# Hybrid decoder step on one core: gate squares summed before the ones product, low parts by adding DMAs, readouts on ScalarE

## The chip, the cores and the metric

The kernel runs on one core of one Trainium2 chip. The host lays arrays out and nothing more, and the program is launched once. The metric is the device time of that core in microseconds (us): before the change 984.8 us, the median of three runs from 984.1 to 984.87.

## The reference, cut to what matters

One inference step of a decoder trunk: 512 prompt tokens and 8 sampled tokens (520 columns in all) of width 1024 go through a feed-forward network (FFN), a mixer and a second FFN, each added to the residual stream `h`. The change lies in the mixer. Its parts:

```python
proj = h @ w_in
u_pool, z, xbc, dt_raw = jnp.split(proj, ...)        # 512, 1024, 1536, 16 columns
pool_out, new_pool = _pool_mix(u_pool, ...)
xbc_act, new_conv = _causal_conv(xbc, ...)
xs, Bm, Cm = jnp.split(xbc_act, ...)
y, h_new = _ssd_scan(xs_h, dt, A, Bm, Cm, h0, chunk)
y = y + d_skip[:, None] * xs_h
y = y.reshape(b, T, SSD_DIM) * jax.nn.silu(z)
yg = y.reshape(b, T, SSD_GROUPS, SSD_DIM // SSD_GROUPS)          # 2 groups of 512
yg = yg * lax.rsqrt(jnp.mean(yg * yg, axis=-1, keepdims=True) + EPS)
y = yg.reshape(b, T, SSD_DIM) * ssd_norm
cat = jnp.concatenate([pool_out, y], axis=-1)
return cat @ w_out, ...
```

For a sampled token the scan is one step: `y_off` is the old state (16 heads of 64 x 128) times the row `C` of its group, summed over the 128 state columns, and scaled by a decay.

## The kernel before, in words

Everything is feature-major: 128 features on the partitions, the 520 columns along them, taken in two halves of 260. Products are made in three passes: a weight and an input are each split into a high part, rounded to the type that TensorE multiplies in one pass (`F32R`), and the low rest; `mm3` (L121) then issues high x high (L122), high x low (L125) and low x high (L126).

A weight of 128 x 1024 is a unit. `load_unit` (L116) brings it with one DMA of SyncE into a half of a `raw` pair (two pairs, so four halves) and calls `split` (L101): ScalarE copies it to `whi` (L106), and VectorE subtracts to get `wlo` (L113). `whi` and `wlo` have three buffers each. `split` has a second way, which the FFNs' weights use for half of their columns: with `late` given, ScalarE writes the negated raw weight, rounded, into `wlo` (L109), and a DMA issued by GpSimd adds the weight from HBM to it (L110).

The mixer runs as stages from two written plans, CONV_PLAN and GATE_PLAN, and a last one that overlaps with the second FFN. The stages that matter here:

- `z` (`zproj`, L1046): eight units of the input projection for the gate z, 48 matmuls each, evacuated by VectorE into `zs`.
- `o`, `g`, `h` (`wout`, L1053): twelve units of the output weights, four for each third of the concatenated input: the pooling part `catp`, then gate groups 0 and 1 (`catg`). 48 matmuls each, added into `h` by VectorE (L1061).
- `A`, `B` (`ssd_a`, `ssd_b`): the scan, a chunk of 128 tokens of one group at a time. GpSimd makes `xw` (L1011), which the state product `pst` (L1024) reads, and scales the running state (L1033).
- `s` (`samples`, L1097): the readouts of sampled tokens. `sample(b, g)` (L906) loads a broadcast row C as `cb` and four state blocks as `h0`, and VectorE multiplies and sums each block in one instruction with an accumulator output into a column of `ysm` (L913): 16 calls, 64 instructions.
- `G` (`gate`, L1067): finishes `ysm` for the group (`sample_y`), takes the silu of z, adds the sampled tokens' readouts (L1075) and multiplies into `zs` (L1077).
- `H` (`gate_out`, L1079): ScalarE squares the group's four tiles of `zs` into `X` (L1083). `rstd` (L165) then lets TensorE multiply each by a matrix of ones and accumulate (L168), which sums over the partitions and puts the sum on all of them; a square root (L169) and a reciprocal (L170) follow. VectorE scales (L1090), ScalarE writes the high part of `catg` (L1091) and VectorE its low part (L1092).

The plans fix the order in which the stages are traced. A planner then simulates the program with its own costs and writes each engine's instruction order from that; on the chip, each engine runs its list in order. The instructions inside `keep_in_program_order` stay in traced order on their engine. What waits in an engine's list holds up all that stands behind it there, and this holds for DMAs too: SyncE's list issues the plain loads, GpSimd's list the adding ones.

Of the kernel before, what the change touches and what calls it, by code (L numbers as in the profile page):

```python
# [11 lines left out]
AF = mybir.ActivationFunctionType  # L12
ALU = mybir.AluOpType
# [3 lines left out]
P = 128  # L17
D = 1024
# [43 lines left out]
def tile_trunk_step(ctx: ExitStack, tc: tile.TileContext, ins: dict, outs: dict):  # L62
    nc = tc.nc
# [6 lines left out]
    wp = ctx.enter_context(tc.tile_pool(name="wp", bufs=3, side="right"))  # L70
# [24 lines left out]
    def raw_tile(name):  # L95
        if not half:
            t = raw_pair(name)
            half.extend([t[:, 1], t[:, 0]])
        return half.pop()

    def split(src, n, name, hp, nb, tags, late=None):  # L101
        hi, lo = (hp.tile([P, 1024], F32R, tag=t, bufs=nb, name=f"{t}_{name}")[:, :n] for t in tags)
        h, l = hi, lo
        if len(src.shape) == 3:
            h, l = (t.rearrange("p (j c) -> p j c", j=src.shape[1]) for t in (hi, lo))
        nc.scalar.copy(h, src)  # L106
        q = 0 if late is None else n - late.shape[1]
        if late is not None:
            nc.scalar.activation(out=lo[:, q:], in_=src[:, q:], func=AF.Copy, scale=-1.0)  # L109
            nc.gpsimd.dma_start(out=lo[:, q:], in_=late, accum_op=ALU.add)  # L110
        if late is None or q:
            s = slice(0, q) if late is not None else slice(None)
            nc.vector.tensor_tensor(out=l[:, s], in0=src[:, s], in1=h[:, s].bitcast(F32), op=ALU.subtract)  # L113
        return hi, lo

    def load_unit(src, n, name):  # L116
        raw = raw_tile(name)[:, :n]
        nc.sync.dma_start(out=raw, in_=src)
        return split(raw, n, name, wp, 3, ("whi", "wlo"))

    def mm3(ps, whi, wlo, xhi, xlo, start, stop, pin=False, **kw):  # L121
        first = nc.tensor.matmul(ps, whi, xhi, start=start, stop=False, **kw)  # L122
# [81 lines left out]
    class Ffn:  # L204
# [257 lines left out]
        def down(self, c, lo, hi, after):  # L462
            n = hi - lo
            banks, units = {}, {}

            def part(d, ks):
                if d not in units:
                    units[d] = load_unit(ins[f"w{self.i}d"][d, :, lo * P : hi * P], n * P, f"{self.i}d{d}_{c}")
                    banks[d] = ps[0].tile([P, 2, 512], F32, tag="BE", bufs=2, name=f"dn{self.i}_{d}_{c}")
                wh, wl = units[d]  # L470
                for b in range(2):
                    for k in ks:
                        g = self.g[lo + k]
                        mm3(banks[d][:, b, :HB], ws(wh, k), ws(wl, k), g[:, 0, b], g[:, 1, b], k == 0, k == n - 1)

            def done(d):
                for b, hs in enumerate(HALVES):
                    nc.vector.tensor_tensor(out=h[:, d, hs], in0=banks[d][:, b, :HB], in1=h[:, d, hs], op=ALU.add)
                    after(d, b, hs)

            part(0, range(n - 1))
            part(1, range(n - 1))
            part(0, range(n - 1, n))
            done(0)
            part(1, range(n - 1, n))
            done(1)
            for d in range(2, KD):
                part(d, range(n))
                done(d)
# [54 lines left out]
    for j in range(KD // 2):  # L544
        for d in (j, j + KD // 2):
            q = slice(NVEC + d * NT if d else 0, NVEC + (d + 1) * NT)
# [82 lines left out]
    todo, late = [], []  # L629
# [48 lines left out]
def mixer(tc, ins, outs, e):  # L678
    nc = tc.nc
    cst, act, wp, tmp, dr, pool = (e[x] for x in ("cst", "act", "wp", "tmp", "dr", "pool"))  # L680
    ones = e["ones"]
    bank, load_unit, mm3, ws, v, rstd, rstds, vec, h, nx2, raw_tile, open_f2, fin, fill = (
        e[x] for x in ("bank", "load_unit", "mm3", "ws", "v", "rstd", "rstds", "vec", "h", "nx2", "raw_tile",
                       "open_f2", "fin", "fill"))
# [19 lines left out]
    X = mp.tile([P, NX, NT], F32, tag="X", name="X")  # L704
# [1 line left out]
    npp = mp.tile([P, 4, PAST], F32, tag="npp", name="npp")  # L706
    ncp = mp.tile([P, 12, 3], F32, tag="ncp", name="ncp")

    def inproj(src, name):
        wh, wl = load_unit(src, D, f"in{name}")  # L710
        bs = [bank(f"in{name}{b}") for b in range(2)]
        for b, hs in enumerate(HALVES):
            for k in range(KD):
                mm3(bs[b][:, :HB], ws(wh, k), ws(wl, k), xh[:, k, hs], xl[:, k, hs], k == 0, k == KD - 1)
        return bs
# [111 lines left out]
    def pooling(g):  # L827
        w = WINDOWS[g]
        bs = inproj(ins["w_in"][12 + g], f"p{g}")
        U = cv[0].tile([P, LP], F32, tag="cu", bufs=6, name=f"PU{g}")  # L830
        us = U[:, SAMPLE_P:LP].rearrange("p (b j) -> p b j", j=16)
# [39 lines left out]
    ysm = mp.tile([P, NX, NS], F32, tag="ysm", name="ysm")  # L871
    sbc = mp.tile([P, 2, NS], F32, tag="sbc", name="sbc")
    junk = act.tile([P, NT], F32, tag="acc", name="junk")[:, :P]
    scr_bc = dr.tile([NS, 512], F32, name="scr_bc")

    def rows_bc(b, a, g):
        return scr_bc.rearrange("b (a g n) -> b a g n", a=2, g=2)[b, a, g].unsqueeze(0).to_broadcast([P, P])
# [28 lines left out]
    def sample(b, g):  # L906
        cb = tmp.tile([P, HB], F32, tag="ta", name=f"cb{b}{g}")[:, :P]
        nc.sync.dma_start(out=cb, in_=rows_bc(b, 1, g))
        h0 = mp.tile([P, 4, P], F32, tag="h0", bufs=4, name=f"h0_{b}{g}")
        nc.sync.dma_start(out=h0, in_=ins["state_ssm"][:, b, 4 * g : 4 * g + 4])  # L910
        for q in range(4):
            tc.keep_in_program_order(
                nc.vector.scalar_tensor_tensor(out=junk, in0=h0[:, q], scalar=1.0, in1=cb, op0=ALU.mult, op1=ALU.mult,  # L913
                                               accum_out=ysm[:, 4 * g + q, b : b + 1]))

    def sample_y(g):
        gs = slice(4 * g, 4 * g + 4)
# [128 lines left out]
    def zproj(j):  # L1046
        if not zbox:
            zbox.append(cv[0].tile([P, NX, NT], F32, tag="zs", name="zs"))
        bs = inproj(ins["w_in"][16 + j], f"z{j}")
        for b, hs in enumerate(HALVES):  # L1050
            nc.vector.tensor_tensor(out=zbox[0][:, j, hs], in0=bs[b][:, :HB], in1=r[:, hs], op=ALU.mult)

    def wout(cat, j, d2, fin=None):  # L1053
        wh, wl = load_unit(ins["w_out"][j, d2], 1024, f"wo{j}{d2}")
        for d in (2 * d2, 2 * d2 + 1):
            for b, hs in enumerate(HALVES):
                ps = bank(f"wo{j}_{d}{b}")
                for k in range(4):
                    i = (d % 2) * 4 + k
                    mm3(ps[:, :HB], ws(wh, i), ws(wl, i), cat[:, 0, k, hs], cat[:, 1, k, hs], k == 0, k == 3)  # L1060
                nc.vector.tensor_tensor(out=h[:, d, hs], in0=ps[:, :HB], in1=h[:, d, hs], op=ALU.add)  # L1061
                if fin is not None:
                    fin(d, b, hs)
# [15 lines left out]
    def gate_out(g):  # L1079
        zs = zbox[0]  # L1080
        ry = mp.tile([P, NT], F32, tag="wph", name=f"yr{g}")
        for q in range(4):
            nc.scalar.activation(out=X[:, 4 * g + q], in_=zs[:, 4 * g + q], func=AF.Square)  # L1083
        for b, hs in enumerate(HALVES):
            rstd(ry, [X[:, 4 * g + q, hs] for q in range(4)], hs, 512, f"y{g}{b}")
        cat = cats[g] = xa.tile([P, 2, 4, NT], F32R, tag="xa", bufs=2, name=f"catg{g}")
        for q in range(4):
            i = 4 * g + q
            gn = v("ssd_norm", i)
            nc.vector.tensor_tensor(out=zs[:, i], in0=zs[:, i], in1=ry, op=ALU.mult)  # L1090
            nc.scalar.activation(out=cat[:, 0, q], in_=zs[:, i], func=AF.Copy, scale=gn)  # L1091
            nc.vector.scalar_tensor_tensor(out=cat[:, 1, q], in0=zs[:, i], scalar=gn, in1=cat[:, 0, q].bitcast(F32),  # L1092
                                           op0=ALU.mult, op1=ALU.subtract)
# [3 lines left out]
    def samples(n):  # L1097
        for _ in range(n):
            if smp:
                sample(*smp.pop(0))  # L1100
# [6 lines left out]
    def outs_a():  # L1107
# [4 lines left out]

    stages = {
        "b": lambda j: conv(8 + j, inproj(ins["w_in"][j], f"bc{j}"), BC[:, j]),
        "x": lambda j: conv(j, inproj(ins["w_in"][4 + j], f"x{j}"), X[:, j]),
        "d": lambda j: box.update(dta=token_dt()) if j == 0 else (token_acs(box["dta"]), sample_decay()) if j == 1 else head_acs(),
# [7 lines left out]
        "A": lambda j: ssd_a(*ssd(j)),  # L1124
        "B": lambda j: ssd_b(*ssd(j)),
        "z": zproj,
        "o": lambda j: wout(catp, 0, j),
        "G": gate,
        "H": gate_out,
        "g": lambda j: wout(cats[0], 1, j),  # L1130
        "h": lambda j: wout(cats[1], 2, j, fin),
        "n": fill,
        "e": lambda j: outs_a(),
# [101 lines left out]
```

## Time and profile before

| | value |
|---|---|
| median of three runs | 984.8 us |
| the profiled execution's own time | 984.47 us |
| its span in the trace | 982.6 us |
| mean granted TensorE clock | 0.997 of full speed |
| mixer's z and output stages, by the trace | about 455 to 640 us of the span |

The profiled execution lies 0.33 us under the median. The trace covers its first to last instruction, 1.87 us less than its time. "Busy" of TensorE counts from a matmul's start to its modelled end, and matmuls overlap, so a row's duration is longer than what the next one waits: the spacing of starts tells what one costs. "Idle before, released by" names the work that ended last before an engine went on. A matmul of plain 32-bit inputs shows as two instructions in the trace.

### The profile page before, as it was taken

How to read it: one execution, taken by the hardware profiler on the slowest of the kernel's cores; microseconds unless marked ns; L12 is line 12 of the kernel's file. 1: busy time of each engine (PE TensorE's matmuls, PEld its weight loads, DVE VectorE, ACT ScalarE, POOL GpSimd, SP SyncE). 2: the span in 40 equal slices, each digit the busy share in tenths (PEclk: the TensorE clock that was granted, in tenths of full speed). 3: DMA queues.
4: the chain of work that ended last, by engine and by line, in shares of the span. 5: the costliest groups of instructions: out<-in, count | busy, mean ns of one | idle time of the engine just before them, and what ended most of it. 6: DMA issues, size and time to landing. Idle time of an engine off the chain costs nothing.

```text
span 982.6 us, 20242 instructions
## 1 busy us (share of the span) xinstructions
PE 951.5 (97%) x7636; PEld 927.4 (94%) x7636; DVE 877.8 (89%) x1624; ACT 678.2 (69%) x1263; POOL 217.9 (22%) x319
## 2 busy tenths in 40 slices
PE   7999999999999999999999999999999999999995
PEld 6899999999999999999899998989999999999995
DVE  7899899989989698788979987999999999999976
ACT  7677677677777475685754335678788888888864
POOL 0112211121121000157411000113333233233300
PEclk9999999999999999999999999999999999999998
DMA  5565766576566243262335232456687768767732
GB/s 182 161 172 114 191 161 143 133 186 175 124 149 165 65 148 119 87 210 86 115 120 165 96 115 90 106 152 164 164 213 185 183 156 223 190 155 189 190 91 88
DMA packets 63571, 145.46 MB, mean 148 GB/s; under 512 B 9257, under 2 KB 22505, under 8 KB 63473
## 3 DMA queue, kind: packets, MB, share of 16 engines
q1 hardware_dynamic: 41168, 103.78, 33.2%
q0 software_dynamic: 22304, 40.38, 22.5%
q8 instruction: 60, 0.98, 0.4%
q14 instruction: 39, 0.31, 0.1%
HBM read 136.80 MB, written 7.34 MB: 147 GB/s over the span
## 4 chain that ended last, share of the span: by engine, by line
PE 85%; DVE 8%; ACT 3%; issue 2%; DMA 1%; POOL 1%; SPq 0%; DVEq 0%; ACTq 0%
PE A L126 7%; PE A L122 7%; PE A L125 7%; PE BE L122 6%; PE BE L125 6%; PE BE L126 6%; PE P L311 3%; PE wo L122 2%; PE wo L125 2%; PE wo L126 2%; PE inz L122 2%; PE A2d L125 2%; PE A2d L126 2%; PE A1d L125 2%; PE A1d L126 2%
## 5 line engine op out<-in xcount | busy, mean ns | idle before, releaser
L380 ACT COPY ac<-A 128x260 f32<-128x260 f32 x123 | 45.1, 369 | 16.8 <-PE A L126 16.5
L311 PE MATMUL P<-xg_f,raw 128*128 128x260 f32 x192 | 45.9, 398 | 5.5 <-DMA raw<-in_w1gu 5.5
L346 DVE TENSOR_TENSOR s<-raw 128x1024 f32<-128x1024 f32 x41 | 49.8, 1216 | 1.4 <-DMA raw<-in_w2gu 1.4
L311 PEld LDWEIGHTS P<-xg_f,raw 128*128 128x128 f32 x192 | 37.5, 199 | 11.5 <-ACT xg_f L188 5.4
L943 POOL DMA_DIRECT2D out_nss<-hs x32 | 20.6, 643 | 79.2 <-DVE hs L961 74.0
L106 ACT CAST whi_wo<-raw_wo 128x1024 fp32r<-128x1024 f32 x12 | 12.5, 1046 | 36.5 <-issue 9.2
L125 PE MATMUL wo<-catg,whi_wo 128*128 128x260 f32 x128 | 36.4, 285 | 1.3 <-DVE catg L1092 1.3
L122 PE MATMUL wo<-catg,whi_wo 128*128 128x260 f32 x128 | 37.3, 292 | 0.3 <-DVE h L1061 0.3
L122 PE MATMUL inz<-xh_mx,whi_inz 128*128 128x260 f32 x128 | 36.8, 288 | 0.0
L122 PE MATMUL inx<-xh_mx,whi_inx 128*128 128x260 f32 x128 | 36.4, 285 | 0.0
L126 PE MATMUL wo<-catg,wlo_wo 128*128 128x260 f32 x128 | 36.3, 284 | 0.0
L126 PE MATMUL inz<-xh_mx,wlo_inz 128*128 128x260 f32 x128 | 36.2, 283 | 0.0
L126 PE MATMUL inx<-xh_mx,wlo_inx 128*128 128x260 f32 x128 | 36.2, 283 | 0.0
L125 PE MATMUL inz<-xl_mx,whi_inz 128*128 128x260 f32 x128 | 36.2, 283 | 0.0
L125 PE MATMUL inx<-xl_mx,whi_inx 128*128 128x260 f32 x128 | 36.1, 282 | 0.0
L392 DVE TENSOR_TENSOR tg<-BE,ac 128x520 f32<-128x520 f32 x41 | 28.3, 691 | 5.2 <-PE BE L126 5.2
L807 DVE SCALAR_TENSOR_TENSOR A<-U,h,A 128x544 f32<-128x544 f32 x36 | 28.0, 778 | 4.3 <-ACT A L805 3.3
L401 DVE TENSOR_TENSOR tg<-tg,r_f 128x520 f32<-128x520 f32 x41 | 28.4, 694 | 1.3 <-ACT tg L399 1.0
L398 DVE TENSOR_TENSOR tg<-tg,r_f 128x520 f32<-128x520 f32 x41 | 28.4, 692 | 0.1
L347 DVE TENSOR_TENSOR s<-s,raw 128x512 f32<-128x512 f32 x41 | 28.0, 682 | 0.0
L348 DVE TENSOR_TENSOR s<-s,raw 128x512 f32<-128x512 f32 x41 | 27.9, 681 | 0.0
L399 ACT ACTIVATE tg<-tg 128x520 f32<-128x520 f32 x41 | 26.1, 637 | 1.0 <-DVE tg L398 0.9
(1787 smaller groups left out, 4747.4 us busy)
## 6 DMA issues: line engine op xcount, KB each, us to landing
raw<-in_w2gu SPq DMA_DIRECT2D x44, 512.0 KB, 4.9
raw<-in_w1gu SPq DMA_DIRECT2D x42, 512.0 KB, 4.7
raw_1d<-in_w1d SPq DMA_DIRECT2D x24, 384.0 KB, 4.0
raw_2d<-in_w2d SPq DMA_DIRECT2D x24, 384.0 KB, 4.0
raw_wo<-in_w_out SPq DMA_DIRECT2D x12, 512.0 KB, 4.8
ab<-scr_acs SPq DMA_DIRECT2D x8, 512.0 KB, 4.4
h<-in_state_ssm SPq DMA_DIRECT2D x16, 256.0 KB, 3.8
raw_inz<-in_w_in SPq DMA_DIRECT2D x8, 512.0 KB, 4.1
```

Of the source, the lines that this page charges most:

```text
L122: first = nc.tensor.matmul(ps, whi, xhi, start=start, stop=False, **kw)
L125: nc.tensor.matmul(ps, whi, xlo, start=False, stop=False, **kw)
L126: nc.tensor.matmul(ps, wlo, xhi, start=False, stop=stop, **kw)
L311: nc.tensor.matmul(self.banks[f, u][b][:, :HB], ws(self.raw[f][:, u], j + 4 * q), xg[:, slot[q]], start=j == q == 0, stop=j == 3 and q == ...
L346: nc.vector.tensor_tensor(out=s1, in0=diag, in1=up0, op=ALU.add)
L347: nc.vector.tensor_tensor(out=s2[:, 0], in0=s1[:, 1], in1=raw[:, 0, :nb], op=ALU.add)
L348: nc.vector.tensor_tensor(out=s2[:, 1], in0=s2[:, 0], in1=raw[:, 0, nb : 2 * nb], op=ALU.add)
L380: nc.scalar.copy(keep, out[:, :HB])
L392: nc.vector.tensor_tensor(out=tg, in0=self.BE[k][:, :, :HB], in1=a, op=ALU.add)
L398: nc.vector.tensor_tensor(out=tg, in0=tg, in1=r, op=ALU.mult)
L401: nc.vector.tensor_tensor(out=tg, in0=tg, in1=r, op=ALU.mult)
L807: nc.vector.scalar_tensor_tensor(out=A[:, :n], in0=U[:, j : j + n], scalar=w(j), in1=A[:, :n], op0=ALU.mult, op1=ALU.add)
```

## The change

Three edits, all in the mixer.

1. `load_unit` takes a flag `late`; with it, the whole low part is made by ScalarE's negated copy and an adding DMA of GpSimd, and VectorE's subtraction is not issued. The eight z units and the twelve output units set it.
2. In `sample`, VectorE multiplies the four state blocks by the broadcast row in one instruction, in place, and ScalarE sums each block with a copy that has an accumulator output.
3. In `gate_out`, VectorE adds the four squared tiles into the first, and the ones product reads that tile alone.

```diff
-    def load_unit(src, n, name):
+    def load_unit(src, n, name, late=False):
         raw = raw_tile(name)[:, :n]
         nc.sync.dma_start(out=raw, in_=src)
-        return split(raw, n, name, wp, 3, ("whi", "wlo"))
+        return split(raw, n, name, wp, 3, ("whi", "wlo"), src if late else None)
...
-    def inproj(src, name):
-        wh, wl = load_unit(src, D, f"in{name}")
+    def inproj(src, name, late=False):
+        wh, wl = load_unit(src, D, f"in{name}", late)
...
+        tc.keep_in_program_order(
+            nc.vector.tensor_tensor(out=h0, in0=h0, in1=cb.unsqueeze(1).to_broadcast([P, 4, P]), op=ALU.mult))
         for q in range(4):
-            tc.keep_in_program_order(
-                nc.vector.scalar_tensor_tensor(out=junk, in0=h0[:, q], scalar=1.0, in1=cb, op0=ALU.mult, op1=ALU.mult,
-                                               accum_out=ysm[:, 4 * g + q, b : b + 1]))
+            nc.scalar.activation(out=junk, in_=h0[:, q], func=AF.Copy, accum_out=ysm[:, 4 * g + q, b : b + 1])
...
-        bs = inproj(ins["w_in"][16 + j], f"z{j}")
+        bs = inproj(ins["w_in"][16 + j], f"z{j}", True)
...
-        wh, wl = load_unit(ins["w_out"][j, d2], 1024, f"wo{j}{d2}")
+        wh, wl = load_unit(ins["w_out"][j, d2], 1024, f"wo{j}{d2}", True)
...
         for q in range(4):
             nc.scalar.activation(out=X[:, 4 * g + q], in_=zs[:, 4 * g + q], func=AF.Square)
+            if q:
+                nc.vector.tensor_tensor(out=X[:, 4 * g], in0=X[:, 4 * g], in1=X[:, 4 * g + q], op=ALU.add)
         for b, hs in enumerate(HALVES):
-            rstd(ry, [X[:, 4 * g + q, hs] for q in range(4)], hs, 512, f"y{g}{b}")
+            rstd(ry, [X[:, 4 * g, hs]], hs, 512, f"y{g}{b}")
```

## The prediction

> **What bounds the kernel now.** First the page: busy time by engine, and the engines' shares of the chain that ended last.
>
> ```profile
> PE 951.5 (97%) x7636; PEld 927.4 (94%) x7636; DVE 877.8 (89%) x1624; ACT 678.2 (69%) x1263; POOL 217.9 (22%) x319
> PE 85%; DVE 8%; ACT 3%; issue 2%; DMA 1%; POOL 1%; SPq 0%; DVEq 0%; ACTq 0%
> ```
>
> TensorE is the bound over the whole kernel, VectorE second. A mean says little of one stage, so next come the stretches that hold the edited work (z units from 455 us, output units to 630):
>
> ```profile
> core 0: us, PE busy (x) PEld busy (x) DVE busy (x) ACT busy (x) POOL busy (x), PEclk, DMA share, GB/s
> 455.00:475.00 20.00, 18.79 (x160) 16.63 (x159) 18.29 (x36) 12.64 (x26) 13.36 (x23) 1.00 0.29 95
> 475.00:505.00 30.00, 29.58 (x246) 27.48 (x247) 25.16 (x53) 19.52 (x40) 6.32 (x7) 1.00 0.36 115
> 505.00:535.00 30.00, 30.00 (x251) 28.39 (x249) 29.20 (x105) 14.89 (x22) 6.89 (x6) 1.00 0.50 162
> 535.00:565.00 30.00, 30.00 (x245) 28.36 (x245) 30.00 (x73) 12.59 (x16) 2.55 (x2) 1.00 0.27 89
> 565.00:600.00 35.00, 31.86 (x243) 30.35 (x243) 29.70 (x84) 11.26 (x16) 0.61 (x1) 1.00 0.33 111
> 600.00:640.00 40.00, 39.05 (x267) 36.66 (x266) 32.74 (x50) 25.58 (x37) 3.71 (x5) 1.00 0.37 106
> ```
>
> VectorE is full from 505 to 565, and yet TensorE has no gap there. So VectorE's time is worth only the gaps that TensorE does have: 3.14 us in 565 to 600 (35.00 less 31.86), and little elsewhere. The waits of TensorE from 455 to 640 us say who ended them (total, times, longest):
>
> ```profile
> PE psr_y L168 <- ACT X L1083: 1.6, 1, 1.6
> PE wo L125 <- DVE catg L1092: 1.3, 2, 0.6
> ...
> PE px L984 <- DVE xdt L1008: 0.7, 1, 0.7
> PE pb L976 <- DVE U L721: 0.6, 1, 0.6
> PE yd L1027 <- DVE U L719: 0.4, 1, 0.4
> PE wo L122 <- DVE h L1061: 0.3, 1, 0.3
> ```
>
> The first two and the last are one story, gate group 1; the timeline shows it:
>
> ```profile
> 575.63 0.29 DVE L913 SCALAR_TENSOR_TENSOR junk<-h,cb 128x128 f32<-128x128 f32 x1
> ...
> 578.35 2.60 ACT L1083 ACTIVATE X<-zs 128x520 f32<-128x520 f32 x4
> ...
> 585.41 1.78 DVE L170 RECIPROCAL yr<-yr 128x260 f32<-128x260 f32 x1 [3.34 <-ACT yr L169]
> ...
> 598.55 0.39 PE L125 MATMUL wo<-catg,whi_wo 128*128 128x260 f32 x1 [0.63 <-DVE catg L1092]
> ```
>
> The last readout ends at 575.9, only then can the gate be finished and squared, and TensorE waits for the squares and, 17 us later, for the low part of `catg`. Group 1's gate is late because its readouts share a full VectorE. Two levers then: TensorE's own work, and these gaps.
>
> **Part 1, the ones product.** The trace has 32 instructions of it, 16 for a group. Group 0's run in one block:
>
> ```profile
> 541.99 3.67 PE L168 MATMUL psr_y<-X,ones 128*128 128x260 f32 x16
> 545.30 0.47 PE L122 MATMUL wo<-catp,whi_wo 128*128 128x260 f32 x1
> 545.61 0.28 PE L125 MATMUL wo<-catp,whi_wo 128*128 128x260 f32 x1
> ```
>
> From 541.99 to 545.61 are 3.62 us, less 0.12 for the one matmul between (the spacing of its neighbours, 571.66 and 571.78 below): 3.50 us for 16. The change leaves 4 of 16, so 2.63 us go, in each of two groups: **5.25 us off TensorE**. TensorE has no gap around 542, so this comes off the end unless a new wait takes it. Bounds: 4.97 by the spacing inside the block (3.31/16 for each of 24), 5.6 if the second group, which ran in four pieces with a change of type around each, saves some changes too.
>
> What it adds are three additions on VectorE in each group, priced by the multiplication of the same size (L1077). The squares are ready one by one, so two additions lie beside later squares (0.63 each) and the last one adds about 0.7 us to the gate's path; three quarters of the ones product, some 2.6 us, leave that path.
>
> **Parts 2 and 3 on VectorE, ScalarE and GpSimd.** The groups, with mean ns of one:
>
> ```profile
> L113 DVE TENSOR_TENSOR wlo_wo<-raw_wo,whi_wo 128x1024 fp32r<-128x1024 f32 x12 | 14.6, 1216 | 0.6 <-ACT whi_wo L106 0.5
> L113 DVE TENSOR_TENSOR wlo_inz<-raw_inz,whi_inz 128x1024 fp32r<-128x1024 f32 x8 | 10.8, 1351 | 1.1 <-ACT whi_inz L106 1.1
> L913 DVE SCALAR_TENSOR_TENSOR junk<-h,cb 128x128 f32<-128x128 f32 x64 | 19.5, 305 | 0.8
> L913 DVE DVE_READ_ACCUMULATOR junk<-h,cb 128x1 f32 x64 | 5.1, 79 | 0.0
> L1037 DVE TENSOR_TENSOR E<-yo,E 128x512 f32<-128x512 f32 x6 | 4.1, 677 | 0.0
> L1077 DVE TENSOR_TENSOR zs<-X,zs 128x520 f32<-128x520 f32 x8 | 5.2, 690 | 0.0
> L106 ACT CAST whi_wo<-raw_wo 128x1024 fp32r<-128x1024 f32 x12 | 12.5, 1046 | 36.5 <-issue 9.2 <-PE wo L125 8.9 <-PE inz L125 8.2
> L979 ACT COPY bt<-pb 128x128 f32<-128x128 f32 x6 | 1.5, 257 | 1.0 <-PE pb L977 1.0
> L960 ACT ACTIVATE so<-br,sxdt 128x128 f32<-128x128 f32 x24 | 9.4, 390 | 0.0
> ```
>
> VectorE loses 14.6 + 10.8 of subtractions and 19.5 + 5.1 of readouts, and gains 16 multiplications of 128 x 512 (0.68 each, 10.9) and six additions (4.1): 35 us less between 455 and 605. By itself that shortens nothing, since TensorE sets the pace; it lets the gate start earlier. Group 1's readouts took 8 x 4 x 0.384 = 12.3 us of VectorE and now take 5.4, and the subtractions between them are gone, so the squares can come several us earlier than 578 and the path to `catg`, which missed by 0.6 us twice, ends in time. Of the 1.6 + 1.3 + 0.3 us of group 1 I take **2.5 us** back (bounds 0, if the planner packs the lists as tightly again, and 3.2). Of the three early waits (0.7 + 0.6 + 0.4, all on VectorE, with two of z's subtractions near them) I take **0.5** (bounds 0 and 1.7).
>
> ScalarE gains 20 negated copies of the cast's size (1.05 each, 21 us) and 64 readouts, which no row shows: from below, the copy of 128 x 128 at 0.257; from above, the one with a scale from memory plus an accumulator read as on VectorE, 0.390 + 0.079 = 0.47. The new one has a constant scale, so it is nearest the first plus the read: 0.34, or 22 us (16 to 30). From 505 to 600 us ScalarE is free 95 less 38.7, so 56 us; 13 of the casts lie there, so 14 us of negated copies, and 22 to 30 of readouts: it holds, with some 12 to 20 us over.
>
> GpSimd gains 20 issues, each waiting in its list for a negated copy, with the scan's `xw` and state scaling behind it. The tightest reader:
>
> ```profile
> 506.92 1.89 POOL L1011 TENSOR_TENSOR xw<-xdt,we 128x512 f32<-128x512 f32 x1 [13.40 <-DVE xdt L1008]
> 512.40 1.02 PE L1024 MATMUL pst<-xw,bt 128*128 128x512 f32 x2
> ```
>
> It has 3.6 us to spare (508.8 to 512.4), against an issue of 0.9; covered. If that cover goes, TensorE stalls there.
>
> **Part 2, when the low part is there.** Until now it came 2.3 us or more after the cast began. Now: cast 1.05, negated copy 1.05, issue 0.9, landing. The adding DMA of the FFNs moves at most 256 KB, this one 512; first its landing over all 126 in the kernel and one issue, then two plain loads, then the cast with the least time to the first use of its unit's low part:
>
> ```profile
> L110 POOL DMA_DIRECT2D wlo_4a<-in_w2gu x1: 888/888/888, 651.7 to 651.7; - x1
> DMA to landing us min/median/max: 3.4/4.9/9.2
> raw_wo<-in_w_out SPq DMA_DIRECT2D x12, 512.0 KB, 4.8
> raw_2d<-in_w2d SPq DMA_DIRECT2D x8, 256.0 KB, 3.0
> ```
> ```profile
> 560.12 1.05 ACT L106 CAST whi_wo<-raw_wo 128x1024 fp32r<-128x1024 f32 x1 [6.83 <-issue]
> ...
> 571.66 0.28 PE L125 MATMUL wo<-catg,whi_wo 128*128 128x260 f32 x1
> 571.78 0.28 PE L126 MATMUL wo<-catg,wlo_wo 128*128 128x260 f32 x1
> ```
>
> A plain load of twice the size lands 1.8 us later, so I take 4.9 + 1.8 = 6.7 us (bounds 3.4, and twice the slowest, 18.4). The chain is then 3.0 + 6.7 = 9.7 us against 11.7 at the tightest unit (560.12 to 571.78): no stall, and none until a landing of 8.7. So this edit costs TensorE nothing, and I add **1.0 us** for small new waits (bounds 0 and the loss in the third rival).
>
> Two rules of the Trainium skill bear on that landing. "DMA: Bandwidth & Descriptors", Anatomy of one DMA, fits a GpSimd-issued DMA by 2.0 us plus the bytes over 436 GB/s, which would be an estimate of 3.2 us here; this trace has no adding DMA under 3.4 us, at half the size or less, so the row decides, and by the page the slack would only grow. "SBUF — State Buffer", on the port pair that VectorE shares with GpSimd, warns that descriptors wait while VectorE holds it and gives 620 ns grown to 3100; here an issue took 888 ns beside a VectorE that was nearly always busy. Were the page's figure true of each, the chain would be about 11.9 us by that estimate, 0.2 late at one unit.
>
> The sum: 5.25 + 2.5 + 0.5 - 1.0 = 7.25 us off 984.47, the profiled execution's own time, gives 977.2. The median lies 0.33 higher, so 977.5 against it; I say 977.3.
>
> **The rivals.** *Only the ones product counts.* The planner writes all lists anew from its own costs, the gaps of group 1 come back elsewhere, and two us of new waits come with them: 984.47 - 5.25 + 2 = 981.2. For it: both groups' waits stem from the order, not from a full engine (VectorE itself idled 3.34 us before the reciprocal). Against: the readouts end earlier.
>
> *The sum of squares stands in VectorE's way.* TensorE's list puts the ones product where the planner expects the last addition; if VectorE is 2.6 us behind in each group, the 5.25 us become waits: 984.5, no change. For it: VectorE was full around 542. Against: it is relieved of 35 us.
>
> *Late low parts, slower.* With three buffers, a unit that is x us late at the tight pace costs x/3 for each unit. The tight stretch holds six units (565 to 600 us at 5.8 us each), so the loss is 2 x (landing - 8.7). From a landing of 12.3 us it is 7.2, more than the 5.25 saved by 2 us; at 16 us it is 14.6, and the time 984.47 - 5.25 + 14.6 = 993.8. For it: single adding DMAs took 9.2 us at half the size. Against: the median, and a DMA share of 0.27 to 0.50 here, to which 20 x 0.5 MB are added. (A readout of 0.8 us on ScalarE would come out alike: 64 of them fill its 42 free us at 0.66.)
>
> **How the numbers follow.** The forecast 0.62, only the ones product 0.19, no change 0.08, slower 0.11. The forecast's own range is 974.5 (all bounds in its favour, 5.25 + 3.2 + 1.7 = 10.1) to 979.5. With the others 974 to 986, which leaves out about 0.05 below and 0.09 above. A measurement of this kernel can tell about 0.2%, 2 us, from no change. Faster: the first two cases, 0.81, less a tail, 0.80; same 0.09; slower 0.11.
>
> **What would show it.** Right: eight instructions of the ones product instead of 32; VectorE some 35 us less busy between 455 and 605, with TensorE still full; the wait for the squares and those for `catg` gone; adding DMAs landing in 5 to 9 us and no TensorE wait on them. Wrong: TensorE waiting at L126 for a DMA of `wlo`, ScalarE readouts over 0.5 us, `pst` waiting for GpSimd, or new gaps in the second FFN, whose order I have taken as unchanged.

## The result, and the profile after

| | before | after |
|---|---|---|
| median of six runs each, same chip, us | 984.55 (983.59 to 986.07) | 992.38 (990.82 to 994.43) |
| ratio, with its 95% interval | | 1.0076 (1.0066 to 1.0087) |
| the profiled execution's own time, us | 984.47 | 991.58 |
| its span in the trace, us | 982.6 | 989.5 |
| mean granted TensorE clock | 0.997 | 0.99 |

The change made the kernel 7.8 us slower: another sign than forecast, and outside the range.

The page of the kernel after, busy time by engine and the shares of the chain:

```profile
PE 949.7 (96%) x7612; PEld 926.0 (94%) x7612; DVE 854.3 (86%) x1498; ACT 720.1 (73%) x1411; POOL 233.2 (24%) x339
PE 76%; DVE 12%; ACT 5%; issue 4%; DMA 1%; POOL 1%; DVEq 0%; SPq 0%; ACTq 0%; POOLq 0%
```

TensorE has 24 instructions fewer, as meant. VectorE's edited rows shrink by 35 us, as meant too (50.0 us of subtractions and readouts gone, 10.5 of multiplications and 4.2 of additions new), but its busy time falls by only 23.5 us in the whole kernel and by 25.1 from 455 to 605 us (134.50 to 109.40): its other rows grew by some 5 us, and busy time, which counts overlapping rows once, falls by less than their sum. Yet TensorE's share of the chain fell by nine points, and VectorE's rose by four. TensorE's waits from 455 to 640 us (total, times, longest) say where:

```profile
PE psr_y L168 <- DVE X L1085: 12.0, 2, 8.1
PE yd L1027 <- DVE U L719: 1.2, 1, 1.2
PE px L984 <- DVE xdt L1008: 1.0, 1, 1.0
PE inz L122 <- DVE E L1037: 0.7, 1, 0.7
```

Line numbers are those of the kernel shown: after the change L1085 is the additions, L912 a readout's multiplication on VectorE and L914 its sum on ScalarE. The first row is new: twice TensorE stands before the ones product (L168) and waits for the additions. The waits of before for the squares and for `catg` are gone; three early ones sum to 2.9 us. The stretches of the same kernel (columns as in the prediction's fence):

```profile
505.00:535.00 30.00, 30.00 (x257) 29.07 (x256) 19.91 (x36) 28.16 (x87) 10.24 (x9) 1.00 0.87 216
535.00:565.00 30.00, 26.12 (x204) 23.67 (x204) 26.40 (x51) 20.36 (x39) 5.06 (x5) 0.94 0.77 191
565.00:600.00 35.00, 26.92 (x202) 26.33 (x201) 22.91 (x48) 22.39 (x66) 3.45 (x4) 0.85 0.62 142
```

TensorE is as full as before until 535 us, then lacks 3.9 us in 535 to 565 and 8.1 us in 565 to 600. The granted clock, third from the right, is 0.94 and 0.85 there, where it was 1.00. The output stage begins 0.9 us later than before (536.10 to 537.01, the first matmul on `catp`), its last `catg` matmul starts 7.4 us later (629.18 to 636.57), and the second FFN's matmuls are all moved by that same 7.4 us (the spans differ by 6.9, for the work behind TensorE's last matmul is 0.5 us shorter). So the loss lies between 537 and about 595 us, and the second FFN has no part in it.

**Group 0.** TensorE and VectorE in the timeline after (start, duration, what, idle before and its releaser):

```profile
542.78 0.28 PE L126 MATMUL wo<-catp,wlo_wo 128*128 128x260 f32 x1
546.94 2.10 PE L168 MATMUL psr_y<-X,ones 128*128 128x260 f32 x4 [3.88 <-DVE X L1085]
```
```profile
541.71 0.69 DVE L1085 TENSOR_TENSOR X<-X 128x520 f32<-128x520 f32 x1
542.32 1.14 DVE L1041 SCALAR_TENSOR_TENSOR X<-X,h,E 128x128 f32<-128x128 f32 x4
543.37 1.29 DVE L912 TENSOR_TENSOR h<-h,cb 128x512 f32<-128x512 f32 x2
...
544.91 0.69 DVE L1085 TENSOR_TENSOR X<-X 128x520 f32<-128x520 f32 x1
...
546.19 0.69 DVE L1085 TENSOR_TENSOR X<-X 128x520 f32<-128x520 f32 x1
```

VectorE has no gap there. The three additions take 2.1 us, but work of the scan, the readouts and the output stands between them in VectorE's list, so from the start of the first to the end of the last are 5.2 us. TensorE came to its product at 542.90 and stood for 4.0 us.

**Group 1.** TensorE, then ScalarE, then VectorE:

```profile
581.01 0.28 PE L126 MATMUL wo<-catg,wlo_wo 128*128 128x260 f32 x1
589.37 2.10 PE L168 MATMUL psr_y<-X,ones 128*128 128x260 f32 x4 [8.08 <-DVE X L1085]
...
591.49 0.42 PE L125 MATMUL wo<-catg,whi_wo 128*128 128x260 f32 x1
591.70 0.42 PE L126 MATMUL wo<-catg,wlo_wo 128*128 128x260 f32 x1
```
```profile
578.70 1.03 ACT L106 CAST whi_wo<-raw_wo 128x1024 fp32r<-128x1024 f32 x1
...
579.95 1.04 ACT L109 ACTIVATE wlo_wo<-raw_wo 128x1024 fp32r<-128x1024 f32 x1
...
581.96 0.19 ACT L914 ACTIVATION_READ_ACCUMULATOR junk<-h 128x1 f32 x1
583.92 0.64 ACT L1083 ACTIVATE X<-zs 128x520 f32<-128x520 f32 x1 [1.77 <-DVE zs L1077]
584.46 1.03 ACT L106 CAST whi_wo<-raw_wo 128x1024 fp32r<-128x1024 f32 x1
585.39 1.05 ACT L109 ACTIVATE wlo_wo<-raw_wo 128x1024 fp32r<-128x1024 f32 x1
586.35 1.67 ACT L1083 ACTIVATE X<-zs 128x520 f32<-128x520 f32 x3
```
```profile
576.30 1.33 DVE L912 TENSOR_TENSOR h<-h,cb 128x512 f32<-128x512 f32 x2 [3.21 <-DMA h<-in_state_ssm]
...
587.00 2.31 DVE L1085 TENSOR_TENSOR X<-X 128x520 f32<-128x520 f32 x3 [0.62 <-ACT X L1083]
```

Read backwards: the last addition ends at 589.31, 1.3 us after the last square. The squares start at 583.92 (before: 578.35) and stand apart by one unit's cast and negated copy. The last readout ends at 582.15 (before: 575.9); it, too, had a cast and a negated copy among its last few, and it waited for the last state loads, which let VectorE begin only at 576.30. The gate's path now runs through ScalarE, and there each unit of weights takes 1.9 us of it where it took 0.95.

Those two loads were issued late, and landed late. SyncE's queue after and before, ScalarE after, and the landing after of the state loads (median over all 16; 3.8 us before) and of the adding DMAs:

```profile
565.92 1.88 SPq L118 DMA_DIRECT2D raw_wo<-in_w_out  x2
...
568.81 1.94 SPq L910 DMA_DIRECT2D h<-in_state_ssm  x2
```
```profile
565.02 0.42 SPq L910 DMA_DIRECT2D h<-in_state_ssm  x1
...
567.01 0.42 SPq L910 DMA_DIRECT2D h<-in_state_ssm  x1
```
```profile
563.89 1.05 ACT L106 CAST whi_wo<-raw_wo 128x1024 fp32r<-128x1024 f32 x1 [4.23 <-PE wo L125]
564.85 1.05 ACT L109 ACTIVATE wlo_wo<-raw_wo 128x1024 fp32r<-128x1024 f32 x1
```
```profile
wlo_wo<-in_w_out POOLq DMA_DIRECT2D x12, 512.0 KB, 7.8
h<-in_state_ssm SPq DMA_DIRECT2D x16, 256.0 KB, 7.1
```

TensorE, late from group 0, frees a `whi` late; ScalarE's cast and negated copy end at 565.90, which frees the raw half; at 565.92 SyncE can issue the next weight load, and the last state loads stand behind it in its list. Before, the last two state loads were issued at 565.02 and 567.01. The longer landing goes with edit 2: the median of the state loads is 3.7 to 4.5 us in the six kernels without it and 5.5 to 7.8 in the eight with it.

**The clock.** The same kernel in stretches of 2 us, granted clock in the third field from the right:

```profile
545.00:547.00 2.00, 0.06 (x1) 0.06 (x1) 2.00 (x5) 1.92 (x7) 0.00 (x0) 0.87 0.31 65
547.00:549.00 2.00, 2.00 (x5) 1.61 (x6) 0.22 (x1) 1.98 (x7) 0.23 (x1) 0.50 0.44 131
...
589.00:591.00 2.00, 1.63 (x5) 1.34 (x5) 0.32 (x1) 0.36 (x1) 0.00 (x0) 0.50 0.81 158
...
593.00:595.00 2.00, 2.00 (x13) 2.00 (x13) 2.00 (x3) 0.00 (x0) 0.00 (x0) 0.68 0.00 0
```

In both idle times TensorE was granted half its clock, and it kept that for some us after work began again: in the fence of group 1 the next matmuls start 0.21 and 0.22 us apart after 591.49, against 0.12 at full clock.

**Where the time went.** Between the start of the output stage and its last matmul the loss is 7.4 - 0.9 = 6.5 us. Into it go -5.25 (the 24 instructions, as forecast), -3.2 (the old waits of group 1, all gone) and +12.0 (the new wait): +3.5. The other 3 us, by difference, are put down to the half clock. Counted by the spacings it cost 3.9 us. From the product's start to L125 are 2.1 us in both groups, where y2_early_reads below takes 1.00 at full clock, and the next 4 matmuls of group 0 and 13 of group 1 were about 0.1 us too far apart: 1.5 and 2.4 us. So this account closes to about 1 us.

### The profile page after: what moved, and what is told of

The parts are those of the page before. It is cut to its first block, busy times and chain, and to the rows that moved or that the text cites. A ratio compares the mean times of both kernels' runs of the same rounds, so it can differ in the third digit from the quotient of the medians.

```text
span 989.5 us, 20291 instructions
## 1 busy us (share of the span) xinstructions
PE 949.7 (96%) x7612; PEld 926.0 (94%) x7612; DVE 854.3 (86%) x1498; ACT 720.1 (73%) x1411; POOL 233.2 (24%) x339
## 4 chain that ended last, share of the span: by engine, by line
PE 76%; DVE 12%; ACT 5%; issue 4%; DMA 1%; POOL 1%; DVEq 0%; SPq 0%; ACTq 0%; POOLq 0%
PE A L126 7%; PE A L122 7%; PE A L125 7%; PE BE L122 5%; PE BE L125 5%; PE BE L126 5%; PE P L311 3%; PE A1d L125 2%; PE A1d L126 2%; PE A1d L122 2%; PE A2d L125 2%; PE A2d L126 2%; PE A2d L122 2%; PE wo L122 1%; PE inx L122 1%
## 5 line engine op out<-in xcount | busy, mean ns | idle before, releaser
L125 PE MATMUL wo<-catg,whi_wo 128*128 128x260 f32 x128 | 36.8, 287 | 0.0
L125 PE MATMUL inz<-xl_mx,whi_inz 128*128 128x260 f32 x128 | 36.1, 282 | 0.0
L125 PE MATMUL inx<-xl_mx,whi_inx 128*128 128x260 f32 x128 | 36.1, 282 | 0.0
L1061 DVE TENSOR_TENSOR h<-wo,h 128x260 f32<-128x260 f32 x48 | 19.2, 419 | 11.6 <-PE wo L126 11.5
```

What stands on the lines that cost most here:

```text
L125: nc.tensor.matmul(ps, whi, xlo, start=False, stop=False, **kw)
```

## The experiments

Each was timed beside the kernel before, in three sets: x1, x2, x3 and x12 (before: 984.58 us), x13, x23, y1 and y2 (985.12), and w1, z1, z2 and z3 (985.14); a ratio is to the kernel before of its own set. Edits 1, 2 and 3 are numbered as the parts of the prediction: sums on VectorE, low parts by adding DMAs, readouts on ScalarE ("The change" lists them as 3, 1 and 2).

| kernel | edits | median us | ratio (95%) | last readout ended | TensorE at group 1's product | it started |
|---|---|---|---|---|---|---|
| before | none | | | 575.9 | 577.3 | 579.0 |
| x1_sum | 1 | 986.58 | 1.0020 (1.0009 to 1.0032) | 577.0 | 577.6 | 584.6 |
| x2_low | 2 | 988.96 | 1.0040 (1.0025 to 1.0056) | 581.1 | 581.0 | 583.9 |
| x3_read | 3 | 979.84 | 0.9954 (0.9941 to 0.9968) | 572.7 | 577.3 | 577.3 |
| x12_sum_low | 1, 2 | 985.72 | 1.0016 (1.0004 to 1.0028) | 574.7 | 576.3 | 582.1 |
| x13_sum_read | 1, 3 | 985.96 | 1.0007 (0.9997 to 1.0016) | 575.1 | 580.2 | 584.7 |
| x23_low_read | 2, 3 | 989.24 | 1.0043 (1.0026 to 1.0059) | 581.2 | 585.6 | 585.6 |
| after | 1, 2, 3 | 992.38 | 1.0076 (1.0066 to 1.0087) | 582.2 | 581.1 | 589.4 |
| w1_five_states | 1, 2, 3, a fifth state slot | 990.95 | 1.0065 (1.0048 to 1.0082) | 581.9 | 583.3 | 589.1 |
| y1_late_ones | 1, 2, 3, product later | 986.91 | 1.0013 (1.0002 to 1.0024) | 575.1 | 585.1 | 585.1 |
| y2_early_reads | 1, 2, 3, readouts earlier | 976.30 | 0.9911 (0.9896 to 0.9926) | 567.4 | 576.9 | 576.9 |
| z1_sum_read_early | 1, 3, readouts earlier | 981.98 | 0.9977 (0.9966 to 0.9987) | 568.0 | 576.4 | 580.2 |
| z2_before_early | none, readouts earlier | 981.59 | 0.9966 (0.9953 to 0.9978) | 570.4 | 576.7 | 576.7 |
| z3_sum_low_early | 1, 2, readouts earlier | 978.18 | 0.9931 (0.9909 to 0.9954) | 565.8 | 577.4 | 577.4 |

The last three columns are read from each kernel's timeline (us from the start of its span). "TensorE at group 1's product" is when TensorE came to it: the start of the matmul before the product plus 0.12. In the traces of before, of after and of every kernel whose plan is unchanged, 48 output matmuls stand ahead of group 0's product in TensorE's list and 288 ahead of the first of group 1's: edits and planner move neither place. With the product 48 matmuls further down (y1_late_ones) it is 96 and 336.

### Edit 1 alone

```diff
             nc.scalar.activation(out=X[:, 4 * g + q], in_=zs[:, 4 * g + q], func=AF.Square)
+            if q:
+                nc.vector.tensor_tensor(out=X[:, 4 * g], in0=X[:, 4 * g], in1=X[:, 4 * g + q], op=ALU.add)
...
-            rstd(ry, [X[:, 4 * g + q, hs] for q in range(4)], hs, 512, f"y{g}{b}")
+            rstd(ry, [X[:, 4 * g, hs]], hs, 512, f"y{g}{b}")
```

> Edit 1 alone: squares summed on VectorE, one ones product per half; low parts and readouts as before. Theory A (the ones product keeps its place in TensorE's list, 48 and 288 output matmuls into the output stage, and TensorE stands there until the last addition is done): VectorE is full, so the additions come late; a wait on L1085 of 0 to 4 us at group 0 and about 5 us at group 1 (squares end at 581, additions at 582 to 583, TensorE is there at 577), some 2 to 3 us more at a lowered clock after them; 5.25 saved: 983 to 988 us. Rival B (the additions are harmless, the adding DMAs or the readouts make the loss): 979 to 981 us, no wait of TensorE on L1085 over 1 us.

Measured: 986.58 us, slower by 2.0. TensorE's wait for L1085 is 9.4 us in two parts, the longest 6.9. Its timeline at group 1:

```profile
584.59 2.10 PE L168 MATMUL psr_y<-X,ones 128*128 128x260 f32 x4 [6.87 <-DVE X L1085]
```

The readouts ended only 1.1 us later than before. The 24 instructions were saved, and the wait for the sum took more than that: the first of four squares had been enough for TensorE to start; now it needs the last square and three additions. From the last readout to the start of the product are 3.1 us before (579.0 less 575.9) and 7.6 here.

### Edit 2 alone

```diff
-        return split(raw, n, name, wp, 3, ("whi", "wlo"))
+        return split(raw, n, name, wp, 3, ("whi", "wlo"), src if late else None)
...
-        bs = inproj(ins["w_in"][16 + j], f"z{j}")
+        bs = inproj(ins["w_in"][16 + j], f"z{j}", True)
...
-        wh, wl = load_unit(ins["w_out"][j, d2], 1024, f"wo{j}{d2}")
+        wh, wl = load_unit(ins["w_out"][j, d2], 1024, f"wo{j}{d2}", True)
```

> Edit 2 alone: low parts of z and output weights by negated copy and adding DMA; sum of squares and readouts as before. Theory A: no low part is late, VectorE is relieved of 25 us, group 1's squares come a little earlier; 982 to 985 us, at most one TensorE wait on the squares of under 2 us. Rival B: the adding DMAs delay the state loads (median landing over 6 us instead of 3.8) and with them the last readout; the last readout ends after 577 and the time is 986 us or more.

Measured: 988.96 us, slower by 4.4; the gain that the main theory expected did not come. No low part is late. The readouts end 5 us later than before, at 581.1, and TensorE itself is late: its output stage begins 3.6 us later than before (539.75 against 536.10). Early in the z stage three waits on VectorE come close together (1.1, 1.0 and 0.7 us from 474 to 478), and the clock falls behind them:

```profile
475.00:485.00 10.00, 8.29 (x58) 7.69 (x55) 9.84 (x23) 8.54 (x22) 4.53 (x7) 0.83 0.50 121
```

Before, TensorE started 79 matmuls in that stretch, here 58, at a granted clock of 0.83. The kernel after has three such waits too, and its clock did not fall there; the last section comes back to this. State loads took 6.5 us to land, weight loads up to 10.6.

### Edit 3 alone

```diff
+        tc.keep_in_program_order(
+            nc.vector.tensor_tensor(out=h0, in0=h0, in1=cb.unsqueeze(1).to_broadcast([P, 4, P]), op=ALU.mult))
         for q in range(4):
-            tc.keep_in_program_order(
-                nc.vector.scalar_tensor_tensor(...
+            nc.scalar.activation(out=junk, in_=h0[:, q], func=AF.Copy, accum_out=ysm[:, 4 * g + q, b : b + 1])
```

> Edit 3 alone: one multiplication on VectorE, four sums on ScalarE at 0.5 us each; the rest as before. Theory A: the place of the ones product is the same, so the time goes by the end of the last readout: at 576 or earlier 983 to 985 us, and for each us that it ends later up to one us more. Rival B (readouts on ScalarE are the cause): the last readout ends about 580 or later, group 1's squares wait, 987 us or more.

Measured: 979.84 us, faster by 4.7: better than any theory. The readouts end at 572.7, 3.2 us earlier, and group 1's product, still of four tiles, runs in one block, with no idle time before it:

```profile
577.32 3.67 PE L168 MATMUL psr_y<-X,ones 128*128 128x260 f32 x16
```

So the gaps of group 1 (3.2 us before) are most of what edit 3 takes back, as the prediction had it for the whole change: its last `catg` matmul starts 4.4 us earlier than before (624.82 against 629.18). The profiled run took 983.14 us against the median of 979.84, so no term is read from its span.

### Edits 1 and 2; 1 and 3; 2 and 3

The diffs above, two at a time.

> Edits 1 and 2, readouts as before on VectorE. Theory A: as edit 1 alone with a VectorE that is 25 us freer, so the additions follow the squares closely; wait at group 0 under 2 us, at group 1 3 to 5 us; 981 to 985 us. Rival B: loads late by the adding DMAs, 987 us or more.

> Edits 1 and 3, low parts by VectorE as before. Theory A (the ones product stands at a fixed place in TensorE's list; the loss is how much later than that the last addition ends; loads at their old landing time let the readouts end early): the readouts end near 573 as with edit 3 alone, additions near 578, wait of TensorE on L1085 of 0 to 3 us in all, 975 to 979 us. Rival C (the additions by themselves cost 2 us or more, wherever they stand, as in edit 1 alone): 981 us or more, wait on L1085 over 5 us.

> Edits 2 and 3, ones product over four tiles as before. Theory A: the state loads land late beside the adding DMAs (median near 7 us) and the readouts end near 581, so TensorE waits for the first squares of group 1 by 3 to 6 us and runs at a lowered clock after it: 986 to 991 us. Rival (edit 1's additions carry the loss): 980 to 984 us.

Measured: 985.72, 985.96 and 989.24 us. With edits 1 and 2, group 0 has no wait (its additions were done at 541.06), and group 1 waits 5.6 us, where 3 to 5 were expected; the time is 0.7 us above the expected range. With 1 and 3, both groups wait, 7.1 us in all, though the readouts end at 575.1: edit 3's gain is lost to edit 1. That fell outside the main theory's 975 to 979 and inside its rival's. With 2 and 3 the product does not wait at all, and the number fell where it was expected, but not for the reason given, a wait for the squares: here a low part is late, the prediction's third rival, once.

```profile
578.40 0.39 PE L126 MATMUL wo<-catg,wlo_wo 128*128 128x260 f32 x1 [4.62 <-DMA wlo_wo<-in_w_out]
```
```profile
568.26 0.87 POOL L110 DMA_DIRECT2D wlo_wo<-in_w_out  x1 [7.56 <-ACT junk L914]
```

The matmuls ahead of it had run to 573.50. The adding DMA was issued at 568.26 and its data used at 578.40; the slowest landing in this kernel is 10.1 us. In the kernel after, no matmul waited for one.

### Is it the place of the product, or the lateness of the sum?

Two changes of the written plan with all three edits. In the first, stage `H` stands one output unit further down in both groups; in the second the readouts (`s2`) are traced earlier:

```diff
-    "A4 z0 B3 z1 m3 z2 B4 z3 s2 A5 z4 s2 B5 A6 z5 s2 s2 G0 z6 A7 z7 B6 s2 o0 H0 s2 o1 B7 s2 o2 s2 G1 "
-    "o3 g0 g1 H1 g2 g3"
+    "A4 z0 B3 z1 m3 z2 B4 z3 s2 A5 z4 s2 B5 A6 z5 s2 s2 G0 z6 A7 z7 B6 s2 o0 s2 o1 H0 B7 s2 o2 s2 G1 "
+    "o3 g0 g1 g2 H1 g3"
```

> All three edits, and both ones products one output unit later (96 and 336 output matmuls ahead of them instead of 48 and 288). Theory A: TensorE works 5.8 us before it gets there, so the wait of 4.0 at group 0 goes and that of 8.1 at group 1 falls to 2 to 3, with little or no time at a lowered clock; in return the output units of group 1 wait for the low part of catg by up to 4 us: 983 to 988 us instead of 992. Rival (TensorE is late by work or by loads, not by the place): 991 to 994 us.

```diff
+    "A4 z0 B3 z1 m3 z2 s2 B4 z3 s2 A5 z4 s2 B5 A6 s2 z5 G0 s2 z6 A7 s2 z7 B6 s2 o0 H0 s2 o1 B7 o2 G1 "
+    "o3 g0 g1 H1 g2 g3"
```

> All three edits, and the readout stages 2 to 8 traced earlier, so that group 1's loads and sums come ahead of the output units. Theory A: the last readout ends before 575, group 1's wait of 8.1 us falls to 3 or less, group 0's stays within 2 us of 4: 982 to 987 us. Rival (the readouts' end does not set group 1's gate, or earlier loads only displace the weights'): 990 us or more.

Measured: 986.91 and 976.30 us. With the product later, the wait for L1085 is gone and 5.5 us of the loss with it (992.38 less 986.91), but what follows the product is late in turn: TensorE waits for `catg` (2.6 and 1.2 us) and for VectorE's evacuation (2.4), in a profiled run of 983.27 us against the median of 986.91. This kernel does not test the place alone: its lists are new too, its readouts end 7 us earlier than in the kernel after, and its sum is ready at 583.45 instead of 589.31. With the sum at 589.31, TensorE, there at 585.1, would still have stood some 4 us, by an estimate from these times. With the readouts earlier all three edits together are the fastest kernel of the study, 8.8 us under before, further than expected. Squares, additions and product of its group 1:

```profile
569.51 2.47 ACT L1083 ACTIVATE X<-zs 128x520 f32<-128x520 f32 x4 [0.21 <-DVE zs L1077]
```
```profile
573.79 0.69 DVE L1085 TENSOR_TENSOR X<-X 128x520 f32<-128x520 f32 x1
```
```profile
576.87 1.04 PE L168 MATMUL psr_y<-X,ones 128*128 128x260 f32 x4
...
577.87 0.28 PE L125 MATMUL wo<-catg,whi_wo 128*128 128x260 f32 x1
```

The sum is there 2.4 us before TensorE comes for it. From the product's start to L125, less 0.12, are 0.88 us for four instructions, against 3.50 for sixteen: 2.62 us saved in a group, where 2.63 was forecast.

### What of that is the plan, and what the edits?

The plan of y2_early_reads, with the kernel before and with two of the edits.

> The kernel before with the readouts traced early and nothing else. Theory A: TensorE has the 5.25 us of the ones product still, and of its waits of 3.2 us at group 1 most go: 981.5 to 984 us. Rival (the plan, not the three edits, makes all of the gain): 976 to 978 us.

> Edits 1 and 3 with the readouts traced early, low parts by VectorE as before the change. Theory A: the readouts end near 567, group 1's additions before TensorE gets there at 577, no wait on L1085 over 1 us, and the early gaps near 474 us are as before the change: 974 to 976.5 us, at or below the same plan with all three edits (976.3). Rival (the adding DMAs are part of the gain): 978 us or more.

> Edits 1 and 2 with the readouts traced early, on VectorE in one instruction each as before. Theory A: if the last readout ends before 568 there is no wait on L1085 over 1 us at group 1: 975.5 to 978 us; group 0's additions stand in a VectorE that has the early readouts too, a wait of up to 4 us there would give 980. Rival (only the readouts on ScalarE make room): 982 us or more.

Measured: 981.59, 981.98 and 978.18 us. The first is inside its expected range, the second far outside it and on its rival's side, the third 0.2 us above. The plan alone brings 3.5 us (985.14 less 981.59) and takes group 1's wait away. The three edits on top of it bring 5.3 us more (981.59 less 976.30; the two stand in different sets, whose kernels before differ by 0.02). Edits 1 and 3 without the adding DMAs bring nothing there: z1_sum_read_early waits 5.9 us at its two products, though its readouts end at 568.0, for its VectorE still makes the low parts, and one of these stands between the additions:

```profile
576.29 0.70 DVE L1085 TENSOR_TENSOR X<-X 128x520 f32<-128x520 f32 x1
...
577.55 1.23 DVE L113 TENSOR_TENSOR wlo_wo<-raw_wo,whi_wo 128x1024 fp32r<-128x1024 f32 x1 [0.22 <-ACT whi_wo L106]
578.70 1.43 DVE L1085 TENSOR_TENSOR X<-X 128x520 f32<-128x520 f32 x2
```

With the adding DMAs (z3_sum_low_early) that subtraction is gone and neither product waits. So, in this plan, edit 1 needs edit 2's relief of VectorE; and without the early readouts the two together are at 985.72 us (x12_sum_low), no faster than before.

### Are the slots of the states what makes the readouts late?

```diff
-        h0 = mp.tile([P, 4, P], F32, tag="h0", bufs=4, name=f"h0_{b}{g}")
+        h0 = mp.tile([P, 4, P], F32, tag="h0", bufs=5, name=f"h0_{b}{g}")
```

> All three edits, and five buffers instead of four for the state blocks of the readouts (and the two small tiles that share them). If the ring of slots (a load of about 7 us, a multiplication, four sums, then the next load may be issued) sets the end of the readouts, group 1's last one ends 2 to 6 us earlier than 582 and the time falls by about as much: 985 to 990 us. If the order of SyncE's list or ScalarE's sums set it, it stays within 1 us of 582 and the time at 991 to 994.

Measured: 990.95 us, and the last readout ends at 581.9, 0.3 us earlier. The slots are not it.

## Why the prediction was wrong, by its own steps

**The ones product: right on TensorE.** The removed work is worth 2.62 us a group where TensorE doesn't wait. The condition beside it, "comes off the end unless a new wait takes it", is the one that failed: new waits took 12.0 us.

**"The squares can come several us earlier than 578": the step that failed.** They came at 583.92, 5.6 us later, and TensorE stood 8.1 us before group 1's product. It was argued from VectorE's relief, which did come (its busy time from 455 to 640 us fell from 165 to 135 us, by the rows of the windows), and edit 3 alone shows that the argument holds while VectorE is the only thing in the way. It left out that all on the gate's path had moved to other queues: readouts and squares share ScalarE's list with each unit's cast and negated copy, the state loads stand in SyncE's list behind a weight load that now waits for ScalarE's negated copy, and they land in 7.1 us instead of 3.8. I had counted whether ScalarE has the time, 12 to 20 us of it to spare, and not whether it has it at 577 to 588.

**The last addition "adds about 0.7 us to the gate's path": mis-sized.** The path to the product was priced from its end. What TensorE waited for before was the first square: it had three more to come while it multiplied. Merging the four into one made it wait for the last square and three additions in a shared list. In x1_sum, where little else moved, that is 4.5 us (7.6 less 3.1 from the last readout to the product). The same merging makes group 0's wait of 4 us in the kernel after, where the squares came only 0.4 us later than before (537.87 against 537.51).

**"1.0 us for small new waits": mis-sized** by 11 us and by the clock, 3 to 4 us more. The early waits did not go back by 0.5 but rose, from 1.7 to 2.9 us.

**The rivals.** The mechanism was the second rival's: TensorE's list has the product at a fixed place and the sum is not ready there. It had a chance of 0.08 and a price of 2.6 us a group; the measured waits are 4 and 8 us. y2_early_reads shows it: the same three edits with the sum made ready first have 0.3 us of that wait. y1_late_ones agrees, but moved the place and the sum at once. The third, late low parts, did not happen in the kernel after: the adding DMAs land in 7.8 us (6.7 taken), under the 8.7 from which it begins at the tightest unit; the slowest took 9.4, and no matmul waited for it. x23_low_read shows that the edge is near.

**Right:** eight instructions; VectorE's relief by the edited rows (35 us, though its busy time from 455 to 605 us fell by 25.1 and TensorE was not full); `pst` never waiting for GpSimd; an unchanged second FFN. **A little off:** a readout on ScalarE takes 0.43 us by the spacing of their starts, where 0.34 was taken (bounds 0.26 to 0.47).

**What stays open.** Why edit 2 alone makes the readouts end at 581 and edits 1 and 2 at 575 is not settled: the early waits, the order of the lists and what waits in them all differ between them. In the kernel after, how much of group 1's lateness is handed on from group 0 (through the late cast and the late loads) was read from the timeline and not tried by itself. The half clock is 3 us by difference and 3.9 by the spacings; no run takes it away alone.

## What to carry to other kernels

Work taken off the engine that sets the pace is worth its time only if what that engine needs next is ready at that place of its list: compare when each input is ready with when the engine arrives, before and after the change. Folding several inputs into one swaps a wait for the first of them for a wait for the last, plus the folding; move the producers earlier along with it (here 16 us between the two plans of the same three edits). And look for the moved work in the lists of the engines and queues that take it, at the time where the path runs through them; a sum over the stage says nothing of that.

## What the runs showed of the hardware that was not expected

A pause of TensorE can cost more than its length, and where it falls counts as well as how long it is. Two kernels, group 0's product of four instructions after a pause of 2.83 us (x1_sum) and of 3.03 us (x13_sum_read), from the start of the matmul before:

```profile
541.95 0.28 PE L126 MATMUL wo<-catp,wlo_wo 128*128 128x260 f32 x1
544.78 1.14 PE L168 MATMUL psr_y<-X,ones 128*128 128x260 f32 x4 [2.56 <-DVE X L1085]
545.58 0.47 PE L122 MATMUL wo<-catp,whi_wo 128*128 128x260 f32 x1
```
```profile
541.62 0.28 PE L126 MATMUL wo<-catp,wlo_wo 128*128 128x260 f32 x1
544.65 2.10 PE L168 MATMUL psr_y<-X,ones 128*128 128x260 f32 x4 [2.75 <-DVE X L1085]
546.18 0.79 PE L122 MATMUL wo<-catp,whi_wo 128*128 128x260 f32 x1
```

The same four took 0.80 us in the one and 1.53 us in the other. The Trainium skill, "TensorE: Matmul & The Clock Gate", What's actually happening, says that the clock is halved after at least one idle window of about 3.4 us and comes back after about as long a busy one, on windows that run freely. The half clock and a return after some us agree (4.9 us from 589.37 in the kernel after, when the spacing is 0.12 again); the pause that was enough here is shorter than the page's window.

The traces' clock records say more. Between 100 and 900 us of the fourteen traces there are 18 stretches at half clock. Each lasts 3.41 us or two or three times that (546.49 to 549.90 and 584.04 to 594.28 in the kernel after), so each trace can be cut into steps of 3.41 us at whose bounds its clock changes. Five such steps, the first three around the two pauses above, the last two around the early waits of the z stage:

| kernel | step, us | TensorE busy, us | idle | clock in the next step |
|---|---|---|---|---|
| x13_sum_read | 540.38 to 543.79 | 1.52 | 55% | half |
| x1_sum | 540.04 to 543.45 | 2.19 | 36% | full |
| x1_sum | 543.45 to 546.87 | 2.08 | 39% | full |
| x2_low | 475.27 to 478.69 | 1.71 | 50% | half |
| after | 474.81 to 478.23 | 1.89 | 45% | full |

The pause of x1_sum fell across two steps and cost no clock; that of x13_sum_read, 0.2 us longer, took more than half of one. In these traces all 18 stretches follow a step that was idle for half of it or more, and of the other steps at full clock one alone was idle for as much (52%, in y1_late_ones).

An adding DMA of 512 KB took 7.8 us to land, and the plain loads of 256 KB among them went from 3.8 to 7.1. An accumulator output on ScalarE shows as an instruction of its own of 187 ns, on VectorE it was 79 ns.
